# Second and third FFN: the first two blocks' activations split behind the third block's weights, and the second FFN's gates scaled behind the last low halves

## The chip, the cores and the metric

The kernel runs on one core of a Trainium2 chip. The metric is the device time of one execution in microseconds (us); lower is better. The time before is 2227.34 us, the median of three runs (2226.12 to 2228.6).

## The reference, cut to what matters

A trunk of four layers works on `x`, 512 positions of 1024 channels in float32. Each layer adds a mixer (S5, gated linear attention, differential attention, S5) and then an FFN with 2816 hidden channels. Only the FFN is touched here:

```python
def swiglu_ffn(h, w_gate_up, w_down):
    g, u = jnp.split(h @ w_gate_up, 2, axis=-1)
    return (jax.nn.silu(g) * u) @ w_down

for layer in range(DEPTH):
    ...
    x = x + mix
    h = rmsnorm(x, norm_ffn[layer])
    x = x + swiglu_ffn(h, ffn_w_gate_up[layer], ffn_w_down[layer])
```

The function `ffn` has an argument `l`, the layer from 0 to 3. The second and third FFN are `l == 1` and `l == 2`.

## The kernel before, in words

**High and low halves.** Every float32 operand of a large product is kept as a high half, rounded to the type that TensorE reads fast, and a low half, the rest. A product is three matmuls: high with high, high with low, low with high. A weight tile (128 partitions x 1024 elements, 512 KB) is staged by a DMA, cast to its high half by ScalarE (`high`, L420), and VectorE subtracts that from the weight to make the low half (`low`, L428). So each weight tile costs one ScalarE and one VectorE instruction before its products can run in full: the first two matmuls of a product need only the high half, the third needs the low one. Five pairs of halves (`whl`) exist at a time.

**A block.** The hidden channels are cut into 11 blocks of 256. A block's gate and up products are made with seven half-sized products instead of eight (`seven_block`, L729). Each product is 24 matmuls of 256 columns (L594), and its left operand is one of the prepared `side` tiles or `sides`. The names in a plan are the products and what is done with their sums: `one` starts a sum in PSUM bank `a`, and `one_out` (L800, ScalarE) copies it to the tile `r1`; `two` goes to bank `d` and `two_out` (L807, VectorE) adds it to `r1`; `five` and `five_out` (L821) make `r5` from bank `c`; `six` adds to bank `a`, once `one_out` has read it, and `six_out` (L835) copies it to `r2`; `seven` adds to `a`, once `six_out` has read it, and `seven_out` (L845) subtracts it from `r5`; `three` adds to `c`, and `three_out` (L852, L853) makes the gated `r1`; `four` adds to `a`. `scale1` and `gate2` (L770) multiply a gate by the rows' norms, `silu1` and `gate2` (L773) apply SiLU, `times` (L865) multiplies with `r5`. `add` (L824) adds one staged quarter of the weights to another, since `six` and `four` use sums: `add22` and then `high1`, `low1` make the operand of `six`, `add21` and then the last halves (`highF`, `lowF`) that of `four`.

**Activations.** Last, `parts` (L867) splits `r1` and `r5` into the high and low halves that the product with `w_down` reads: a ScalarE cast (L877) and a VectorE subtraction (L878) for each. In the third FFN the rows are permuted (`turn`), and each is done in two instructions of half the size. `parts` is also the last reader of `r1`.

**Buffers.** The tiles `r1` have two buffers (tag `r1`), the others three (tag `glu`, both at L734). PSUM has four banks for `a` and `c` and two for `d`.

**Order.** Blocks 1 and 2 ("a" and "b" in the plans) go side by side by a plan, a list of steps written by hand. Blocks 3 to 11 go one by one through the loop at the end of `ffn`. Block 3 is `blocks[2]`. After each group of blocks (4, 4 and 3) the loop `gemm_b` multiplies with `w_down`. Within this order a scheduler that runs when the program is built sets the final order of the instructions on each engine; every engine then runs its own list strictly in that order and waits by semaphores. `issue_after(ins)` binds what is traced under it to stand behind `ins` on the engine of `ins` alone. Weight loads are issued from SyncE, and loads that add to a staged quarter from GpSimd (L759); both wait for free buffers.

Second and third FFN are not `glued`: block 3's first products come out of the loop and not out of a plan, and in the loop `gate2`, `times` and `parts` of blocks 1 and 2 are traced ahead of block 3's steps.

Of the kernel before, what the change touches and what calls it, by code (L numbers as in the profile page):

```python
# [69 lines left out]
class Left:  # L70
# [4 lines left out]
    early = False  # L75
# [79 lines left out]
class Sides(Left):  # L155
# [4 lines left out]
    early = True  # L160
# [180 lines left out]
class Trunk:  # L341
# [544 lines left out]
    def ffn(self, l, left, after=None, turn=False, aside=None, small=None):  # L886
# [7 lines left out]
        with self.tc.tile_pool(name=f"ffn{l}", bufs=1, reuse_waits="tile") as fp:  # L894
# [3 lines left out]
            glued = l in (0, 3)  # L898
# [8 lines left out]
            blocks = [self.seven_block(fp, slots, left, wgu, b, turn, na, glued) for b in range(FFN_HIDDEN // 256)]  # L907
# [27 lines left out]
            if l == 1:  # L935
                a = plan.index("seven_out:b")
                plan = plan[:a] + """
                    seven_out:b scale1:a silu1:a scale1:b silu1:b add21a high22 low22 three:b highFa add21b lowFa highFb
                    lowFb four:a four:b three_out:a three_out:b
                """  # L940

            def turned():
# [3 lines left out]
            def loads(b=blocks[2]):  # L946
                for w in ("direct", "room1", "room22", "room21", "summed"):
                    b[w]()
# [22 lines left out]
            for nb in (4, 4, 3) if na == 4 else (3, 3, 3, 2):  # L971
                acts = []
                for n in range(b0, b0 + nb):
                    b = blocks[n]
                    if not glued and n < 2:
                        if l == 2 and n == 0:
                            loads()
                            blocks[2]["split"]("1")
                        if l == 2 and n == 1:
                            for step in ("one", "one_out", "five", "five_out"):  # L980
                                blocks[2][step]()
                            blocks[2]["add"]("22")
                            blocks[2]["split"]("1")
                        for step in ("gate2", "times"):
                            b[step]()
                    if n > 2 or l == 1 and n == 2:
                        loads(b)
                        for step in ("one", "one_out", "five", "five_out"):
                            b[step]()
                        b["add"]("22")  # L990
                    if n > 1:
                        for step in ("six", "six_out", "two", "two_out", "scale1", "silu1", "seven", "seven_out", "three", "three_out"):
                            b[step]()
                        b["add"]("21")
                        for step in ("four", "gate2", "times"):
                            b[step]()
                    with self.tc.issue_after(behind["low"].ins) if glued and n < 2 else nullcontext():
                        acts.append(b["parts"]())
                stat = lambda k, part, t: acts[k // 2][:, part, k % 2, t * P : (t + 1) * P]
                if b0 + nb == 11:  # L1000
                    if l == 0:
                        nxt = Sides(self, after, None, i["gla_w_in"][0], lambda half, b: GLA_COLS[b] + half * 256, True)
                    else:
                        nxt = (Chunks if turn else Last if l == 3 else Left)(self, after)
                for d in range(2):
                    tail = 4 if d == 1 and b0 + nb == 11 else 0
                    self.gemm_b(stat, wd, 2 * nb, d * 512, self.add_x(d, nxt, r), k0=2 * b0, tail=tail, jobs=jobs,
                                behind=None if d or l == 0 else dict(self.last),
                                ahead=(lambda: self.gla_ahead(nxt)) if tail and l == 0 else None,
                                middle=(lambda: nxt.total("3")) if tail and l == 0 else None)  # L1010
                b0 += nb
# [1916 lines left out]
```

## Time and profile before

| what | value |
|---|---|
| median of three runs | 2227.34 us |
| profiled execution, its own time | 2228.83 us |
| its span, first to last instruction | 2227.1 us |
| granted TensorE clock, mean | 0.998 |
| VectorE busy | 1631.7 us (73%) |
| ScalarE busy | 1145.4 us (51%) |
| second FFN, end of the plan and blocks 3 and 4 | about 800 to 856 us |
| third FFN, the same | about 1424 to 1470 us |

The profiled execution took 2228.83 us, of which 2227.1 lie between the first and the last instruction. Its rows are read so: the start in us from the span's start, the duration, the engine (PE is TensorE's matmuls, DVE VectorE, ACT ScalarE, POOL GpSimd), the line, the operation, out<-in by the program's names, the size, how often it stands in this row, and in brackets how long the engine stood idle before it and for whom. A matmul's duration includes its way through the array, so two starts tell more than one duration.

### The profile page before, as it was taken

How to read it: one execution, taken by the hardware profiler on the slowest of the kernel's cores; microseconds unless marked ns; L12 is line 12 of the kernel's file. 1: busy time of each engine (PE TensorE's matmuls, PEld its weight loads, DVE VectorE, ACT ScalarE, POOL GpSimd, SP SyncE). 2: the span in 40 equal slices, each digit the busy share in tenths (PEclk: the TensorE clock that was granted, in tenths of full speed). 3: DMA queues.
4: the chain of work that ended last, by engine and by line, in shares of the span. 5: the costliest groups of instructions: out<-in, count | busy, mean ns of one | idle time of the engine just before them, and what ended most of it. 6: DMA issues, size and time to landing. Idle time of an engine off the chain costs nothing.

```text
span 2227.1 us, 38431 instructions
## 1 busy us (share of the span) xinstructions
PE 2166.7 (97%) x15409; PEld 1964.6 (88%) x15409; DVE 1631.7 (73%) x2504; ACT 1145.4 (51%) x1844; POOL 332.2 (15%) x443
## 2 busy tenths in 40 slices
PE   6999999999999999999999999999999999999998
PEld 5888989989988898999888888999998888989997
DVE  9965878777988597876745676967766965957675
ACT  8644635444665465564435675644544234635343
POOL 3401142440210010100002221100000001101000
PEclk9999999999999999999999999999999999999999
DMA  4357667664863676764238455975631646856532
GB/s 93 64 173 179 174 156 188 178 172 157 187 149 114 160 193 164 178 187 124 95 130 167 108 133 150 252 193 143 180 94 48 171 142 152 208 152 170 162 76 76
DMA packets 309220, 333.75 MB, mean 150 GB/s; under 512 B 70452, under 2 KB 253008, under 8 KB 308914
## 3 DMA queue, kind: packets, MB, share of 16 engines
q1 hardware_dynamic: 239010, 239.07, 35.0%
q0 software_dynamic: 70032, 92.23, 22.0%
q8 instruction: 121, 1.98, 0.4%
q14 instruction: 57, 0.47, 0.1%
HBM read 297.29 MB, written 18.75 MB: 142 GB/s over the span
## 4 chain that ended last, share of the span: by engine, by line
PE 79%; DVE 10%; ACT 5%; issue 3%; DMA 1%; POOL 1%; SPq 0%; DVEq 0%; POOLq 0%; ACTq 0%
PE a L594 20%; PE acc L448 11%; PE acc L450 11%; PE acc L449 11%; PE c L594 10%; PE d L594 6%; DVE whl L428 2%; PE y L1670 2%; ACT whl L420 2%; PE acc L1706 2%; PE op L2711 1%; PE s L2678 1%; PE tp L117 1%; PE V L1626 1%; PE acc L2766 1%
## 5 line engine op out<-in xcount | busy, mean ns | idle before, releaser
L428 DVE TENSOR_TENSOR whl<-wst,whl 128x1024 fp32r<-128x1024 f32 x260 | 316.4, 1222 | 214.9 <-ACT whl L420 213.5
L594 PE MATMUL a<-side,whl 128*128 128x256 f32 x3240 | 393.4, 278 | 7.2 <-DVE whl L428 6.8
L420 ACT CAST whl<-wst 128x1024 fp32r<-128x1024 f32 x260 | 272.1, 1052 | 239.3 <-PE acc L450 152.8
L594 PEld LDWEIGHTS a<-side,whl 128*128 128x128 f32 x3240 | 379.6, 188 | 10.4 <-DVE whl L428 8.4
L448 PE MATMUL acc<-whl,act 128*128 128x512 f32 x704 | 275.8, 392 | 0.0
L449 PE MATMUL acc<-whl,act 128*128 128x512 f32 x704 | 274.5, 390 | 0.0
L450 PE MATMUL acc<-whl,act 128*128 128x512 f32 x704 | 274.5, 390 | 0.0
L594 PE MATMUL c<-side,whl 128*128 128x256 f32 x2160 | 261.4, 277 | 2.1 <-DVE whl L428 1.6
L594 PEld LDWEIGHTS c<-side,whl 128*128 128x128 f32 x2160 | 253.1, 188 | 2.9 <-DVE whl L428 2.0
L428 DVE TENSOR_TENSOR whl<-slot,whl 128x1024 fp32r<-128x1024 f32 x105 | 127.7, 1221 | 61.3 <-ACT whl L420 60.7
L448 PEld LDWEIGHTS acc<-whl,act 128*128 128x128 f32 x704 | 132.2, 188 | 27.9 <-DVE x L576 0.5
L450 PEld LDWEIGHTS acc<-whl,act 128*128 128x128 f32 x704 | 132.2, 188 | 27.7
L449 PEld LDWEIGHTS acc<-whl,act 128*128 128x128 f32 x704 | 132.2, 188 | 26.4
L420 ACT CAST whl<-slot 128x1024 fp32r<-128x1024 f32 x105 | 109.9, 1052 | 83.8 <-PE acc L450 44.6
L594 PE MATMUL a<-sides,whl 128*128 128x256 f32 x1080 | 132.6, 278 | 1.8 <-DVE whl L428 1.1
L594 PE MATMUL d<-sides,whl 128*128 128x256 f32 x1080 | 131.7, 278 | 1.6 <-ACT whl L420 1.6
L420 ACT CAST whl<-halves 128x1024 fp32r<-128x1024 f32 x87 | 91.0, 1051 | 80.3 <-DVE halves L824 31.0
L594 PEld LDWEIGHTS a<-sides,whl 128*128 128x128 f32 x1080 | 128.0, 188 | 3.1 <-DVE whl L428 1.4
L428 DVE TENSOR_TENSOR whl<-halves,whl 128x1024 fp32r<-128x1024 f32 x87 | 105.7, 1221 | 34.1 <-ACT whl L420 33.7
L594 PEld LDWEIGHTS d<-sides,whl 128*128 128x128 f32 x1080 | 127.7, 188 | 2.1 <-ACT whl L420 2.1
L759 POOL DMA_DIRECT2D wst<-in_ffn_w_gate_up_dram x44 | 57.0, 1296 | 446.1 <-DMA wst<-in_ffn_w_gate_up_dram 179.3
L877 ACT CAST act<-r 128x512 fp32r<-128x512 f32 (+1 forms) x110 | 66.1, 642 | 101.3 <-DVE r L853 83.7
(530 smaller groups left out, 4025.2 us busy)
## 6 DMA issues: line engine op xcount, KB each, us to landing
wst<-in_ffn_w_gate_up_dram SPq DMA_DIRECT2D x88, 512.0 KB, 4.8
wst<-in_ffn_w_down_dram SPq DMA_DIRECT2D x88, 512.0 KB, 4.6
slot<-in_ffn_w_gate_up_dram SPq DMA_DIRECT2D x69, 512.0 KB, 6.0
wst<-in_ffn_w_gate_up_dram POOLq DMA_DIRECT2D x44, 512.0 KB, 6.0
halves<-in_ffn_w_gate_up_dram SPq DMA_DIRECT2D x42, 512.0 KB, 6.8
wst<-in_s_w_glu_dram SPq DMA_DIRECT2D x32, 512.0 KB, 4.9
wst<-in_diff_w_qkv_dram SPq DMA_DIRECT2D x24, 512.0 KB, 4.1
slot<-in_ffn_w_gate_up_dram POOLq DMA_DIRECT2D x18, 512.0 KB, 8.5
```

Source lines behind the costliest of these rows:

```text
L117: tr.nc.tensor.transpose(p[:, j], h[:, j * P : (j + 1) * P], tr.ident[:])
L420: self.last["high"] = self.nc.scalar.copy(hl[:, 0], w[:])
L428: self.last["low"] = self.nc.vector.tensor_tensor(hl[:, 1], w[:], hl[:, 0].bitcast(F32), op=ALU.subtract)
L448: mm(out, lh, rh, start=first, stop=False)
L449: mm(out, lh, rl, start=False, stop=False)
L450: self.last["mm"] = mm(out, ll, rh, start=False, stop=last)
L594: mm(o, *two, start=first and not (j or k or n), stop=k == 3 and n == 2, skip_group_check=True,)
L759: nc.gpsimd.dma_start(w[:], left.quarter(*plus, b), accum_op=ALU.add)
L877: self.last["act high"] = nc.scalar.copy(dst[:, 0, j], src[:, j])
L1626: mm(V[kk][z][:, bs(b)], inm[:, z, bs(b)], U[:, bs(b)], start=True, stop=True)
L1670: mm(yb[:, b], q[:, j, b], om[:, j // 2, bs(b)], start=False, stop=j == 3)
L1706: mm(accs[t][:], zT[:, m // 2, kk, t * P : (t + 1) * P], hl[:, m % 2, kk % 2], start=kk == 0 and m == 0, stop=kk == KT - 1 and m == 2,)
```

## The change

Two things are moved, and nothing is added or left out. In the second FFN's plan `scale1` and `silu1` of both blocks go behind the last low halves (`lowFb`). In the second and third FFN `parts` of blocks 1 and 2 is traced behind block 3's `four`, and bound on VectorE behind block 3's low halves: in the second FFN behind the last of them (that of `four`), in the third FFN block 1's behind that of `seven` and block 2's behind the last.

```diff
             if l == 1:
                 a = plan.index("seven_out:b")
                 plan = plan[:a] + """
-                    seven_out:b scale1:a silu1:a scale1:b silu1:b add21a high22 low22 three:b highFa add21b lowFa highFb
-                    lowFb four:a four:b three_out:a three_out:b
+                    seven_out:b high22 add21a low22 three:b highFa lowFa add21b highFb lowFb scale1:a silu1:a four:a
+                    scale1:b silu1:b four:b three_out:a three_out:b
                 """
...
                     if n > 1:
                         for step in ("six", "six_out", "two", "two_out", "scale1", "silu1", "seven", "seven_out", "three", "three_out"):
                             b[step]()
+                            if step == "seven":
+                                early = self.last["low"]
                         b["add"]("21")
-                        for step in ("four", "gate2", "times"):
+                        b["four"]()
+                        if n == 2 and not glued:
+                            with self.tc.issue_after(early.ins if l == 2 else self.last["low"].ins):
+                                acts.append(blocks[0]["parts"]())
+                            with self.tc.issue_after(self.last["low"].ins):
+                                acts.append(blocks[1]["parts"]())
+                        for step in ("gate2", "times"):
                             b[step]()
+                    if not glued and n < 2:
+                        continue
                     with self.tc.issue_after(behind["low"].ins) if glued and n < 2 else nullcontext():
                         acts.append(b["parts"]())
```

What the built programs hold shows at three places. The first is VectorE (DVE) in the second FFN, right behind `seven_out:b`. `r_8202` and `r_8216` are `r1` of blocks 1 and 2, `lent` holds the quarters that become the operands of `four:a` and `four:b`. Before:

```order
L770 TENSOR_TENSOR r_8202<-r_8202,R 128x512
L770 TENSOR_TENSOR r_8216<-r_8216,R 128x512
L824 TENSOR_TENSOR lent<-lent,slot_8119 128x1024
L241 TENSOR_TENSOR side_8117<-halves,side_8117 128x1024
L824 TENSOR_TENSOR lent<-lent,slot_8120 128x1024
L428 TENSOR_TENSOR whl<-lent,whl 128x1024 x2
```

The same place on VectorE in the changed program:

```order
L824 TENSOR_TENSOR lent<-lent,slot_8119 128x1024
L241 TENSOR_TENSOR side_8117<-halves,side_8117 128x1024
L428 TENSOR_TENSOR whl<-lent,whl 128x1024
L824 TENSOR_TENSOR lent<-lent,slot_8120 128x1024
L428 TENSOR_TENSOR whl<-lent,whl 128x1024
L770 TENSOR_TENSOR r_8202<-r_8202,R 128x512
L770 TENSOR_TENSOR r_8216<-r_8216,R 128x512
```

The two gate scalings moved from the head of this row to its end, and the first low half no longer stands behind the second sum.

The second place is ScalarE (ACT) in the second FFN, around block 3's `one_out`. `r_8641` before and `r_8631` now are block 3's `r1`, `r_8304` and `r_8374` are `r5` of blocks 1 and 2. Before:

```order
L877 CAST act<-r_8304 128x2x256
L773 ACTIVATE g_8595<-g_8595 128x512
L800 COPY r_8641<-a 128x512
L877 CAST act<-r_8374 128x2x256
L420 CAST whl<-halves 128x1024
L420 CAST whl<-slot_8121 128x1024
L821 COPY r_8671<-c 128x512
L420 CAST whl<-wst 128x1024
L420 CAST whl<-halves 128x1024 x2
L835 COPY r_8701<-a 128x512
```

And in the changed program, from the same cast of `r_8304` on:

```order
L877 CAST act<-r_8304 128x2x256
L420 CAST whl<-halves 128x1024
L773 ACTIVATE g_8590<-g_8590 128x512
L420 CAST whl<-slot_8121 128x1024
L420 CAST whl<-wst 128x1024
L821 COPY r_8661<-c 128x512
L420 CAST whl<-halves 128x1024
L877 CAST act<-r_8374 128x2x256
L420 CAST whl<-halves 128x1024
L420 CAST whl<-wst 128x1024
L420 CAST whl<-halves 128x1024
L800 COPY r_8631<-a 128x512
```

Block 3's `one_out` moved from ahead of all casts of block 3's later weights to behind them, and behind two casts of block 4. It now waits, by its semaphores, for the VectorE split of block 1's `r1`, whose buffer it takes over; before it waited only for `one`.

The third place is VectorE in the third FFN, behind `three_out` of block 2. `r_14416` and `r_14430` are `r1` of blocks 1 and 2, `r_14518` and `r_14596` their `r5`. Before:

```order
L853 TENSOR_TENSOR r_14430<-r_14430,r_14653 128x512
L878 TENSOR_TENSOR act<-r_14416,act 128x64x4
L865 TENSOR_TENSOR r_14518<-g_14820,r_14518 128x512
L878 TENSOR_TENSOR act<-r_14416,act 128x64x4
L428 TENSOR_TENSOR whl<-wst,whl 128x1024
L878 TENSOR_TENSOR act<-r_14518,act 128x64x4 x2
L824 TENSOR_TENSOR halves<-halves 128x1024
L878 TENSOR_TENSOR act<-r_14430,act 128x64x4 x2
L428 TENSOR_TENSOR whl<-halves,whl 128x1024
L428 TENSOR_TENSOR whl<-slot_14331,whl 128x1024
L770 TENSOR_TENSOR g_14894<-a,R 128x512
L428 TENSOR_TENSOR whl<-wst,whl 128x1024
```

The same place on VectorE in the changed program:

```order
L853 TENSOR_TENSOR r_14430<-r_14430,r_14653 128x512
L428 TENSOR_TENSOR whl<-wst,whl 128x1024
L865 TENSOR_TENSOR r_14518<-g_14820,r_14518 128x512
L824 TENSOR_TENSOR halves<-halves 128x1024
L428 TENSOR_TENSOR whl<-halves,whl 128x1024
L428 TENSOR_TENSOR whl<-slot_14331,whl 128x1024
L824 TENSOR_TENSOR halves<-halves,slot_14331 128x1024
L428 TENSOR_TENSOR whl<-wst,whl 128x1024
L428 TENSOR_TENSOR whl<-halves,whl 128x1024 x2
L878 TENSOR_TENSOR act<-r_14416,act 128x64x4 x2
L878 TENSOR_TENSOR act<-r_14518,act 128x64x4 x2
L878 TENSOR_TENSOR act<-r_14430,act 128x64x4
```

All five low halves of block 3 from `one` on that are still open there come first, and the split activations (L878) behind them. Here too `one_out` of block 3 now waits for the split of block 1's `r1`.

On TensorE the products of block 3 stand in the order one, five, six, two, seven, three, four before, with the first two matmuls of some pulled ahead. In the changed program they stand as one, five, two, three, six, seven, four, with `one` of block 4 cut into pieces between six, seven and four, and with two matmuls of block 4's `five` ahead of `six` in the second FFN.

## The prediction, as it was put on record

> **What bounds the kernel now.** The page's first part says which engine carries the time:
>
> ```profile
> PE 2166.7 (97%) x15409; PEld 1964.6 (88%) x15409; DVE 1631.7 (73%) x2504; ACT 1145.4 (51%) x1844; POOL 332.2 (15%) x443
> ```
>
> TensorE is busy for 97% of the span. A change that adds no matmul and removes none can only move the time by the moments in which TensorE waits. So I next read the windows around the two places, each line with the window, its length and the busy time of each engine:
>
> ```profile
> 800.00:830.00 30.00, 26.68 (x226) 25.87 (x225) 28.93 (x35) 19.07 (x24) 5.15 (x4) 1.00 1.00 246
> 830.00:860.00 30.00, 30.00 (x249) 29.32 (x248) 23.10 (x28) 14.28 (x21) 2.57 (x2) 1.00 0.73 195
> 1430.00:1450.00 20.00, 17.48 (x144) 16.69 (x144) 19.89 (x27) 13.30 (x19) 3.86 (x3) 1.00 1.13 281
> ```
>
> In the first and the third, VectorE is busy 28.93 of 30 us and 19.89 of 20 while TensorE has holes of 3.3 and 2.5 us. Here VectorE is the bound, and the order of its list decides. Behind it (830 to 860) TensorE is never idle, so what is lost or won before stays to the end.
>
> TensorE's timeline shows the holes. The second FFN, from `four` of blocks 1 and 2 on:
>
> ```profile
> 807.84 0.39 PE L594 MATMUL a<-side,whl 128*128 128x256 f32 x2
> 809.96 5.50 PE L594 MATMUL a<-side,whl 128*128 128x256 f32 x46 [1.73 <-DVE whl L428]
> 815.30 2.88 PE L594 MATMUL a<-sides,whl 128*128 128x256 f32 x24
> 818.02 0.39 PE L594 MATMUL c<-side,whl 128*128 128x256 f32 x2
> 819.51 2.78 PE L594 MATMUL c<-side,whl 128*128 128x256 f32 x22 [1.10 <-DVE whl L428]
> 822.33 0.50 PE L594 MATMUL a<-side,whl 128*128 128x256 f32 x2
> 823.28 0.50 PE L594 MATMUL d<-sides,whl 128*128 128x256 f32 x2 [0.44 <-ACT whl L420]
> 823.62 2.76 PE L594 MATMUL a<-side,whl 128*128 128x256 f32 x22
> 826.22 2.70 PE L594 MATMUL d<-sides,whl 128*128 128x256 f32 x22
> 828.76 2.88 PE L594 MATMUL a<-side,whl 128*128 128x256 f32 x24
> 831.48 2.88 PE L594 MATMUL c<-side,whl 128*128 128x256 f32 x24
> ...
> 856.00 0.39 PE L448 MATMUL acc<-whl,act 128*128 128x512 f32 x1
> ```
>
> Undisturbed, 24 matmuls take 831.48 - 828.76 = 2.72 us, 0.113 each. What a start lies later than the one before it plus its matmuls is lost: 809.96 - 807.84 - 0.23 = 1.89 before the third matmul of `four:a`, 1.26 before the third of block 3's `five`, then 0.33, 0.72 and 0.11 around `six` and `two`. Sum **4.31 us**. The last row is the first matmul with `w_down`. The third FFN, from block 3's `one` on:
>
> ```profile
> 1428.92 0.39 PE L594 MATMUL a<-sides,whl 128*128 128x256 f32 x2
> 1429.47 2.86 PE L594 MATMUL c<-side,whl 128*128 128x256 f32 x22 [0.16 <-DVE r L852]
> 1433.47 2.86 PE L594 MATMUL a<-sides,whl 128*128 128x256 f32 x22 [1.15 <-DVE whl L428]
> 1436.17 0.40 PE L594 MATMUL c<-side,whl 128*128 128x256 f32 x2
> 1437.77 0.50 PE L594 MATMUL d<-sides,whl 128*128 128x256 f32 x2 [1.21 <-ACT whl L420]
> 1438.26 3.09 PE L594 MATMUL a<-side,whl 128*128 128x256 f32 x24
> 1441.18 2.73 PE L594 MATMUL d<-sides,whl 128*128 128x256 f32 x22
> 1443.76 0.39 PE L594 MATMUL c<-side,whl 128*128 128x256 f32 x2
> 1444.31 3.00 PE L594 MATMUL a<-side,whl 128*128 128x256 f32 x24 [0.17 <-ACT r L835]
> ```
>
> In the same way 0.32, 1.51, 0.21, 1.37, 0.26 and (at 1444.31) 0.32: **3.99 us**. So all that there is to win at both places is about 8.3 us.
>
> **The change part by part.** It removes no instruction, so each list is walked with durations of before. They come from these rows of VectorE, ScalarE and GpSimd:
>
> ```profile
> 802.89 0.68 DVE L845 TENSOR_TENSOR r<-r,a 128x512 f32<-128x512 f32 x1
> 803.49 1.28 DVE L770 TENSOR_TENSOR r<-r,R 128x512 f32<-128x512 f32 x2
> 804.69 1.22 DVE L824 TENSOR_TENSOR lent<-lent,slot 128x1024 f32<-128x1024 f32 x1
> 826.86 2.35 DVE L428 TENSOR_TENSOR whl<-halves,whl 128x1024 fp32r<-128x1024 f32 x2
> 829.13 0.68 DVE L807 TENSOR_TENSOR r<-r,d 128x512 f32<-128x512 f32 x1
> 1429.93 0.68 DVE L853 TENSOR_TENSOR r<-r,r 128x512 f32<-128x512 f32 x1
> 1430.53 0.62 DVE L878 TENSOR_TENSOR act<-r,act 128x256 fp32r<-128x256 f32 x1
> 1431.07 0.68 DVE L865 TENSOR_TENSOR r<-g,r 128x512 f32<-128x512 f32 x1
> 809.83 1.05 ACT L420 CAST whl<-wst 128x1024 fp32r<-128x1024 f32 x1
> 810.79 1.04 ACT L420 CAST whl<-halves 128x1024 fp32r<-128x1024 f32 x1
> 817.82 0.63 ACT L773 ACTIVATE g<-g 128x512 f32<-128x512 f32 x1 [0.64 <-DVE g L770]
> 818.35 0.57 ACT L800 COPY r<-a 128x512 f32<-128x512 f32 x1
> ...
> 1438.58 1.06 ACT L420 CAST whl<-wst 128x1024 fp32r<-128x1024 f32 x1
> 1425.07 1.31 POOL L759 DMA_DIRECT2D wst<-in_ffn_w_gate_up_dram x1 [0.43 <-DVE whl L428]
> ```
>
> A full weight tile on VectorE holds the next one back by (829.13 - 826.86) / 2 = 1.14 and gives its result after 1.22; a 512 one 0.60 and 0.68; the half-sized split 0.54 and 0.62. On ScalarE a cast holds 0.96 and gives its result after 1.05, a 512 one 0.53 and 0.57 to 0.63. Between engines I add 0.03.
>
> *Second FFN, `four` of blocks 1 and 2.* VectorE is free at 803.49 as before. Sum a to 804.71, `side` at 804.63, cast a on ScalarE to 805.79, low a 805.82 to 807.04, sum b 806.96 to 808.18, cast b to 809.26, low b 809.29 to 810.51. TensorE reaches `four:a` at 807.84 and `four:b` at 810.56: both halves are there. **The 1.89 us go.** The two scalings that stood ahead (2 x 0.60) now stand behind, where `three_out`, which needs them, is waited for by nobody at once.
>
> *Second FFN, block 3.* TensorE is early now: `one` at 813.28, `five` at 816.00. On VectorE, 810.43: three 512 instructions, low of `one` 812.23, four 512 ones, low of `five` 815.77 to 816.99. The third matmul of `five` comes at 817.03 instead of 816.23: 0.80 lost. It ends at 819.52. `two` stands next. Its cast on ScalarE is queued behind the cast for `six`, which waits for `add22` (VectorE 817.51 to 818.73), and a SiLU: 818.76, 819.72, 820.25 to 821.30. `two` starts at 821.33: 1.81 lost. Its low half is behind that of `six` and a `times`: 821.58 to 822.80, third matmul 822.83: 1.27 lost. `two` and `three` run through to 828.04. Then block 4's first pieces wait for their casts, which stand behind the cast for `four`, and that for `add21` (VectorE 824.99 to 826.21): 826.24, 827.20, 828.16. Two matmuls at 828.28, two at 829.24. ScalarE copies `one_out` at 829.18 (it also waits for the split of block 1's `r1`, 828.46 to 829.14), to 829.76, and `six` starts at 829.79: 0.24 + 0.74 + 0.33. `six` ends 832.51; two pieces of block 4's `one` wait for their low half to 833.29: 0.81; before `four` about 0.1. The sum is 0.80 + 1.81 + 1.27 + 1.31 + 0.81 + 0.1 = **6.1 us**, against 4.31: **1.8 us lost**. The gain at `four` is eaten, since an earlier TensorE meets the same VectorE and ScalarE lists.
>
> *Third FFN.* The two lists are alike up to VectorE's 1429.93. Then low of `one` 1430.53 to 1431.75, where it was a split with the low half far behind. TensorE has 11 matmuls of `five` (0.32 lost ahead, as before), which end at 1430.72; third of `one` 1431.78: 1.06 lost. `five` ends 1435.74. `times` 1431.67, `add22` 1432.27 to 1433.49, its cast to 1434.57, the low of `six` 1434.60, of `two` 1435.74 to 1436.96; third of `two` 1436.99: 1.02 lost. `add21` 1436.88, lows of `seven`, `three` (1439.16 to 1440.38) and `four` (1440.30): third of `three` 1440.41, 0.70 lost. Only now the splits of `r1`, 1441.44 and 1441.98 to 1442.60; ScalarE's `one_out` to 1443.20, `six` 1443.23: 0.55 lost. Then two splits of `r5`, one of block 2's `r1` and a gate (1444.14 to 1444.82), SiLU, `two_out`, a split, `times` to 1446.55, and on ScalarE two casts of block 2's `r5` ahead of `six_out`: 1446.58, 1447.04, 1447.50 to 1448.10. `seven` could start at 1446.41 and starts at 1448.13: 1.72 lost. `four` waits 0.35 for `seven_out`. Sum 0.32 + 1.06 + 1.02 + 0.70 + 0.55 + 1.72 + 0.35 = **5.7 us** against 3.99: **1.7 us lost**.
>
> The sum: 1.8 + 1.7 = 3.5 us. The profiled execution (2228.83, span 2227.1) would take 2232.3, its span 2230.6; it stands 1.49 above the median, so the median would be 2227.34 + 3.5 = **2230.8 us**. Loads hang on the freed tiles and move with the lists; SyncE issues the same loads, some in another order, and none of the walked steps waits for one. No new kind of work is in the change, so no price is unknown; unknown is how far each of the 15 new joints is off. Counted over all 144 matmuls from 807.84 to 828.76, the second FFN lost 20.92 - 16.32 = 4.60, 0.29 more than its six joints show, 0.05 for each. Between exact and 0.1 more at each new joint the sum is 3.5 to 5.0 us. I take 3.5, since the old joints hide as much and only the difference counts.
>
> A rule of the Trainium skill speaks against my spacing: its page "VectorE: DVE Perf Modes", section "The DRAIN you can't avoid", says that a VectorE instruction starts only when the one before has left the pipe. By the row of two low halves (2.35 for two of 1.22) the second starts 0.08 before the first has ended, so the trace does not bear this out for plain successors. By the rule the sum would be about 5 us (the rival without overlap, below).
>
> **The rivals.** *It is faster.* If block 3's `one_out` in the second FFN ended before TensorE is through `three` at 828.04, 1.7 us sooner than walked, and ScalarE's casts with it, the three waits for low halves (1.89, 1.26 and, in the third FFN, 1.51) would go and none come: 2227.34 - 4.66 = 2222.7. For it: these are the waits that the rows name. Against it: the two buffers of `r1`, and VectorE's full windows; the work is only moved. *Half of that:* only the 1.89 is kept and the rest comes out even, 2225.5 to 2229. *More is lost.* In the third FFN ScalarE's cast of the operand of `seven` (L420 at 1438.58 before) now follows `five_out`, which follows the end of `five` (1435.74), and comes at 1436.3, over 2 us earlier. Its tile is filled by the load that GpSimd issues at 1425.07, and these take
>
> ```profile
> DMA to landing us min/median/max: 6.7/9.9/10.9
> ```
>
> from issue to landing between 1405 and 1450, so it has landed by 1425.07 + 10.9 = 1435.97, 0.3 us ahead. If it lands 2 us late, that cast and the one for `three` behind it hold TensorE for 1 us or more; with 0.1 more at each joint (1.5 us) this gives 2231.8 to 2236. *No overlap on VectorE.* If in the new order each VectorE instruction waited out the 0.08 us that the next one now overlaps, the some 20 in the third FFN's chain up to `six_out` would bring `seven` 20 x 0.08 = 1.6 us later: 2232.4. The pair of low halves above speaks against it. *The clock falls.* Both windows show a granted clock of 1.00 with a hole of 1.89 in them. Were it to fall to a half for some microseconds, each 24 matmuls would take another 2.72 us: with two or more such groups 2236 and above. The Trainium skill, page "TensorE: Matmul & The Clock Gate", section "A second HAM failure mode: psum-queue depth-cycling", says that many short pauses between groups of matmuls can make the clock swing; in this trace it did not. That the change does not do what it says is ruled out by the rows of the built programs.
>
> **How the numbers follow.** 0.2% is 4.45 us and about what a measurement of this kernel can tell from no change. Chances: the forecast (2229 to 2231.8) 0.53; half the gain (2225.5 to 2229) 0.14; more lost (2231.8 to 2236) 0.24; no overlap 0.01; faster 0.06; the clock 0.02. So faster 0.06, within 0.2% 0.53 + 0.14 = 0.67, slower 0.24 + 0.01 + 0.02 = 0.27. The range leaves out the faster case, the clock and the ends of the two beside the forecast: 2226.5 to 2234.5.
>
> **What would show it.** Right: TensorE runs `four` of blocks 1 and 2 in the second FFN without a hole; then holes before `two` (for ScalarE's cast, then for VectorE's low half) of about 1.8 and 1.3; `six` waits for ScalarE's L800 in both FFNs, and that for L878; in the third FFN `seven` waits some 1.7 for L835. TensorE's first matmul with `w_down`, at 856.00 in the second FFN before, comes 1.8 later. Wrong: `six` not waiting for L800, or a wait on a load in either window.

## The result, and the profile after

The changed kernel takes **2233.16 us** (median of 10 runs, 2230.62 to 2236.82) against 2227.74 for the kernel before (10 runs, 2226.12 to 2229.92). The medians lie 5.4 us apart. The ratio of the two kernels' times is put at 1.0020 with a 95% interval of 1.0012 to 1.0028, so the change loses 2.7 to 6.2 us. Forecast was a loss of 3.5, to a median of 2230.8.

The first part of the page of the profiled execution (2234.14 us, span 2232.4), then the windows of two stretches shown of before:

```profile
PE 2171.0 (97%) x15409; PEld 1968.3 (88%) x15409; DVE 1632.0 (73%) x2504; ACT 1145.9 (51%) x1844; POOL 331.9 (15%) x443
...
800.00:830.00 30.00, 26.00 (x214) 24.86 (x214) 27.06 (x33) 16.75 (x22) 3.87 (x3) 1.00 0.98 234
1430.00:1450.00 20.00, 16.18 (x130) 14.99 (x129) 18.70 (x26) 13.86 (x21) 5.16 (x4) 1.00 1.13 303
```

The counts of instructions are those of before. In 800 to 830 TensorE runs 12 matmuls fewer than before (214 against 226) and in 1430 to 1450 it runs 14 fewer. The engine that was full, VectorE, is now **less** busy there: 27.06 against 28.93 us, and 18.70 against 19.89. It did not lose time to more work. It waited.

TensorE in the second FFN, from `four` on:

```profile
806.06 5.64 PE L594 MATMUL a<-side,whl 128*128 128x256 f32 x48
811.54 3.11 PE L594 MATMUL a<-sides,whl 128*128 128x256 f32 x24
814.49 0.39 PE L594 MATMUL c<-side,whl 128*128 128x256 f32 x2
815.41 2.86 PE L594 MATMUL c<-side,whl 128*128 128x256 f32 x22 [0.53 <-DVE whl L428]
819.77 0.50 PE L594 MATMUL d<-sides,whl 128*128 128x256 f32 x2 [1.50 <-ACT whl L420]
821.30 2.86 PE L594 MATMUL d<-sides,whl 128*128 128x256 f32 x22 [1.03 <-DVE whl L428]
...
826.83 0.41 PE L594 MATMUL a<-sides,whl 128*128 128x256 f32 x2
828.18 0.50 PE L594 MATMUL c<-side,whl 128*128 128x256 f32 x2 [0.93 <-ACT whl L420]
828.66 3.00 PE L594 MATMUL a<-side,whl 128*128 128x256 f32 x24
...
856.36 0.39 PE L448 MATMUL acc<-whl,act 128*128 128x512 f32 x1
```

The two `four` run without a hole, as 48 matmuls in one row. Starts less the matmuls between them give 0.69 before the third matmul of `five`, 1.87 and 1.30 around the start of `two` (bank `d`), and 1.12 before block 4's `five`. From the first matmul of `four` to the first one with `w_down` it took 856.36 - 806.06 = 50.30 us. Before it took 856.00 - 807.84 = 48.16, so **2.1 us** are lost here. (The whole trace runs 1.8 us ahead at this place: the trace of before has a stretch of half clock at 262.67, and this one has it later. More of that below.)

TensorE in the third FFN, from block 3's `one` on:

```profile
1430.12 0.39 PE L594 MATMUL a<-sides,whl 128*128 128x256 f32 x2
1430.69 1.54 PE L594 MATMUL c<-side,whl 128*128 128x256 f32 x11 [0.18 <-DVE r L852]
1433.02 2.78 PE L594 MATMUL a<-sides,whl 128*128 128x256 f32 x22 [0.79 <-DVE whl L428]
...
1438.32 2.81 PE L594 MATMUL d<-sides,whl 128*128 128x256 f32 x22 [0.81 <-DVE whl L428]
...
1444.55 3.00 PE L594 MATMUL a<-side,whl 128*128 128x256 f32 x24 [0.27 <-ACT r L800]
...
1447.62 0.39 PE L594 MATMUL a<-sides,whl 128*128 128x256 f32 x2
1449.40 3.00 PE L594 MATMUL a<-side,whl 128*128 128x256 f32 x24 [1.40 <-ACT r L835]
...
1474.15 0.39 PE L448 MATMUL acc<-whl,act 128*128 128x512 f32 x1
```

`six` (1444.55) waits for L800 and `seven` (1449.40) for L835. To the first matmul with `w_down` it is 1474.15 - 1430.12 = 44.03. The row of before that answers is

```profile
1471.45 0.39 PE L448 MATMUL acc<-whl,act 128*128 128x512 f32 x1
```

and 1471.45 - 1428.92 = 42.53, so **1.5 us** are lost here. Below, "the second FFN" and "the third FFN" mean these two stretches, from the same first to the same last matmul.

Now VectorE. These are all of its waits in the two windows, two of them with the sum ahead, and in the third FFN alike:

```profile
805.24 1.22 DVE L824 TENSOR_TENSOR lent<-lent,slot 128x1024 f32<-128x1024 f32 x1
807.66 1.23 DVE L428 TENSOR_TENSOR whl<-lent,whl 128x1024 fp32r<-128x1024 f32 x1 [1.20 <-ACT whl L420]
...
818.28 1.22 DVE L428 TENSOR_TENSOR whl<-halves,whl 128x1024 fp32r<-128x1024 f32 x1 [0.59 <-ACT whl L420]
...
823.44 1.21 DVE L824 TENSOR_TENSOR halves<-halves,slot 128x1024 f32<-128x1024 f32 x1
825.76 1.22 DVE L428 TENSOR_TENSOR whl<-halves,whl 128x1024 fp32r<-128x1024 f32 x1 [1.11 <-ACT whl L420]
```

```profile
1433.49 1.22 DVE L824 TENSOR_TENSOR halves<-halves 128x1024 f32<-128x1024 f32 x1
1435.90 1.23 DVE L428 TENSOR_TENSOR whl<-halves,whl 128x1024 fp32r<-128x1024 f32 x1 [1.20 <-ACT whl L420]
```

All four have one form, the second with one scaling (L770) in between: VectorE makes a sum (L824), ScalarE casts it (L420), VectorE makes the low half (L428). The three hang on one another, and VectorE stands idle for the length of the cast (1.05 us and the ways there and back) unless something else stands in between. Before, the scalings and splits stood in between: 1.0 us of waits in 800 to 830 and none in 1430 to 1450, against 2.9 and 1.2 now. This is the first candidate for the cause. The second is block 3's `one_out` (L800):

```profile
1442.72 2.75 DVE L878 TENSOR_TENSOR act<-r,act 128x256 fp32r<-128x256 f32 x5
```

```profile
1443.91 0.58 ACT L800 COPY r<-a 128x512 f32<-128x512 f32 x1 [1.66 <-DVE act L878]
```

In the third FFN ScalarE is free and waits 1.66 us for the split of block 1's `r1` (the first two of the five), whose buffer `one_out` needs.

### The profile page after: what moved, and what is told of

Same layout as the page of the kernel before. It is cut to its first block, busy times and chain, and to the rows that moved or that the text cites. A ratio compares the mean times of both kernels' runs of the same rounds, so it can differ in the third digit from the quotient of the medians.

```text
span 2232.4 us, 38426 instructions
## 1 busy us (share of the span) xinstructions
PE 2171.0 (97%) x15409; PEld 1968.3 (88%) x15409; DVE 1632.0 (73%) x2504; ACT 1145.9 (51%) x1844; POOL 331.9 (15%) x443
## 4 chain that ended last, share of the span: by engine, by line
PE 80%; DVE 9%; ACT 5%; issue 2%; DMA 2%; POOL 1%; SPq 0%; DVEq 0%; POOLq 0%; ACTq 0%
PE a L594 20%; PE acc L448 11%; PE acc L450 11%; PE acc L449 11%; PE c L594 10%; PE d L594 5%; DVE whl L428 2%; PE y L1680 2%; ACT whl L420 2%; PE acc L1716 2%; PE op L2721 1%; PE s L2688 1%; PE tp L117 1%; PE V L1636 1%; PE acc L2776 1%
## 5 line engine op out<-in xcount | busy, mean ns | idle before, releaser
L428 DVE TENSOR_TENSOR whl<-wst,whl 128x1024 fp32r<-128x1024 f32 x260 | 316.4, 1222 | 215.2 <-ACT whl L420 213.5
L420 ACT CAST whl<-wst 128x1024 fp32r<-128x1024 f32 x260 | 272.2, 1052 | 241.5 <-PE acc L450 154.7
L428 DVE TENSOR_TENSOR whl<-slot,whl 128x1024 fp32r<-128x1024 f32 x105 | 127.7, 1221 | 61.0 <-ACT whl L420 60.9
L420 ACT CAST whl<-slot 128x1024 fp32r<-128x1024 f32 x105 | 109.9, 1052 | 83.5 <-PE acc L450 44.6
L428 DVE TENSOR_TENSOR whl<-halves,whl 128x1024 fp32r<-128x1024 f32 x87 | 105.7, 1221 | 37.8 <-ACT whl L420 37.6
L420 ACT CAST whl<-halves 128x1024 fp32r<-128x1024 f32 x87 | 90.8, 1051 | 78.1 <-DVE halves L824 28.9
```

Of the source, the lines that this page charges most:

```text
L420: self.last["high"] = self.nc.scalar.copy(hl[:, 0], w[:])
L428: self.last["low"] = self.nc.vector.tensor_tensor(hl[:, 1], w[:], hl[:, 0].bitcast(F32), op=ALU.subtract)
```

## The experiments

Three theories are told apart. **The filler**: the moved instructions filled VectorE's waits behind the sums. **The buffer**: the late split of `r1` makes `one_out` late, and `six` and `seven` behind it. **The clock**: the granted clock falls for a few microseconds.

### One part of the change at a time

Only the plan (`e1_plan`):

```diff
-                    seven_out:b scale1:a silu1:a scale1:b silu1:b add21a high22 low22 three:b highFa add21b lowFa highFb
-                    lowFb four:a four:b three_out:a three_out:b
+                    seven_out:b high22 add21a low22 three:b highFa lowFa add21b highFb lowFb scale1:a silu1:a four:a
+                    scale1:b silu1:b four:b three_out:a three_out:b
```

> Only the second FFN's plan is changed (the scalings of blocks 1 and 2 behind the last low half); the split activations stay where they were. Theory 1, the filler: a sum on VectorE, ScalarE's cast of it and the low half of it need one another, so VectorE stands idle for about 1.2 us between sum and low half unless something else stands there; the moved instructions were what stood there. Then VectorE waits 1.2 us between the sum b and its low half, the hole of 1.89 us at the product four of block 1 is gone, and a walk through the lists with the durations of before brings the first matmul with w_down (856.00 before) 0.6 us later: the total is 0.3 to 0.9 us over before. Theory 2, the buffer: what costs is block 3's one_out, which waits for the late split of r1. Here that split is early, so most of the 1.89 us is kept: 1 to 1.9 us under before. Theory 3, the clock: the windows move by less than 0.5 us, and the total follows the number of stretches of half clock, some 1.5 us each.

Measured: 2230.61 us against 2229.76, ratio 1.0005 (0.9996 to 1.0014). The trace has no hole at `four`, but a longer one before the third matmul of block 3's `five`:

```profile
816.60 0.39 PE L594 MATMUL c<-side,whl 128*128 128x256 f32 x2
820.52 4.19 PE L594 MATMUL c<-side,whl 128*128 128x256 f32 x22 [3.53 <-DVE whl L428]
824.54 0.39 PE L594 MATMUL a<-side,whl 128*128 128x256 f32 x2
```

The second FFN loses 1.76 us. Of this some 1.5 are clock: the 22 matmuls from 820.52 take 4.02 us, where 22 x 0.113 is 2.49. Without it 0.2 to 0.3 are left, near the 0.6 of the walk. The 1.89 us are not kept, although `one_out` is early here (818.08), so the buffer alone does not explain the loss.

Only the splits of the second FFN (`e3_parts_second`) and only those of the third (`e4_parts_third`), both with the old plan; here the second, the third has `l == 2`:

```diff
-                        if n == 2 and not glued:
+                        if n == 2 and l == 1:
...
-                    if not glued and n < 2:
+                    if l == 1 and n < 2:
                         continue
```

> Only the split activations of the second FFN are moved; the plan and the third FFN are as before. Theory 1, the filler: VectorE idles ahead of the low half of the operand of six and that of four, where the splits stood; the walk gives 1.2 us later at the first matmul with w_down, total 0.9 to 1.5 over before. Theory 2, the buffer: all that the second FFN loses in the changed kernel comes from here, with the 1.89 us at four still standing: 2.1 + 1.89 = about 4 us over before. Theory 3, the clock: no more than 0.5 us at the first matmul with w_down.

> Only the split activations of the third FFN are moved; the second FFN is as before. Theories 1 and 2 both expect what the changed kernel shows there, 1.6 to 1.8 us over before at the third FFN's first matmul with w_down, and as much in the total if the clock is alike. Theory 3, the clock: 5.4 us of the changed kernel are mostly stretches of half clock that go with any change of order, so the total is 1.7 us plus some 1.5 for each such stretch more than before.

Measured: 2230.73 (ratio 1.0004, 0.9995 to 1.0012) and 2231.41 (1.0003, 0.9994 to 1.0012), against 2229.76. By the traces the one loses 1.28 us in the second FFN and nothing in the third (-0.17), the other 0.00 in the second and 1.74 in the third. The terms sit where the change sits, at the sizes that the walk gives (1.2 and 1.6). Where a kernel leaves a stretch as it was, its trace differs from that of before by 0.00, -0.17 and, in the third FFN of the plan alone, -0.22 us, so differences of some 0.2 us say nothing. By the times alone none of the three parts can be told from no change; their medians sum to a loss of 3.5.

The changed kernel beside them (`c1_after`), and two traces more of it (`c2_after`, `c3_after`):

> The changed kernel once more, beside the others on one chip. Without more stretches of half clock than before: 2.1 + 1.75 = 3.9 us over before. Theory 3, the clock: 5 us or more over before again, with stretches of half clock in the trace that before has not at the same places; if they belong to the change they are at the same places as in the first trace of it (1281, 1752 and 1943 us), if they come and go, at others.

> The changed kernel for another trace. The stretches of half clock last 3.41 us each, and the three of its first trace begin 138.0 and 56.0 times 3.41 us apart. Theory 3a: the clock is judged in fixed stretches of 3.41 us whose beginning is random from run to run, and a stretch in which TensorE was busy for less than about half is followed by one of half clock. Then the pauses at 819 to 822 us (3.2 of 4.3 us idle) bring one at about 820 to 825 in some traces and not in others, and all starts within one trace lie a whole number of 3.41 us apart. Theory 3b: the stretches at 262, 1281, 1752 and 1943 have nothing to do with the change, and the one at 823 was an exception: none at 820 here.

> The changed kernel for a further trace, as the one before: by theory 3a a stretch of half clock at 820 to 825 in about half of such traces, by theory 3b none.

Measured: 2233.61 against 2229.76 (ratio 1.0018, 1.0010 to 1.0027), then single runs of 2233.38 and 2232.47. The four traces of the changed kernel lose in the second FFN 2.14, 3.64, 3.67 and 1.96 us, in the third 1.50, 1.58, 1.43 and 1.76. The two with 3.6 have a stretch of half clock right there. Windows of `c2_after`, cut at its beginning (PEclk is the third column from the end):

```profile
819.16:822.57 3.41, 0.88 (x6) 0.66 (x6) 3.38 (x4) 3.41 (x5) 0.00 (x0) 1.00 0.79 132
822.57:825.98 3.41, 3.41 (x19) 3.41 (x18) 2.98 (x3) 1.34 (x3) 1.28 (x1) 0.50 0.35 57
825.98:829.40 3.42, 3.42 (x31) 3.42 (x30) 2.73 (x4) 1.70 (x2) 0.00 (x0) 1.00 1.04 218
```

In the 3.41 us ahead TensorE was busy for 0.88, because two holes came right after one another; then the clock is halved for 3.41 us (19 matmuls for 31), though TensorE is busy all through. The stretches at other places are as short, follow pauses that both kernels have, and change from trace to trace: 262.67 in the one of before, 1280.70, 1751.74 and 1942.89 in the first of the changed kernel, none of these in the second. The three starts of that trace lie 471.04 and 191.15 apart, 138.0 and 56.0 times 3.413, so the cuts between the stretches run on by themselves, and it is chance on which side of a cut a pause falls. The two traces of the changed kernel without half clock at 820 agree: in the first a cut falls at 819.90, between the two holes, and the 3.41 us on its two sides hold 1.91 and 2.38 us of TensorE's work. So the fixed stretches of theory 3a are borne out, and 3b's "none at 820" falls in one trace of two (`c2_after` has one, `c3_after` none). The row ahead of the stretch in the trace of before, and that of the second trace of the changed kernel (`c1_after`):

```profile
259.26:262.67 3.41, 1.81 (x12) 1.50 (x13) 3.41 (x6) 1.42 (x2) 1.30 (x1) 1.00 0.20 22
```

```profile
819.56:822.97 3.41, 1.81 (x13) 1.61 (x14) 3.41 (x5) 3.41 (x5) 0.64 (x1) 1.00 0.45 75
```

TensorE was idle for 1.6 of 3.41 us, in two pieces in the second case (1.59 and 1.03, of which a part lies in the row), and half clock followed. It need not: theory 3a's "less than about half" is not the whole rule. With all 13 traces cut at this spacing, from 25 to 2200 us, each of the five full-clock stretches with 1.25 us of work or less is followed by half clock, but of those with 1.5 to 2.1 us only 11, and 73 are not. Ahead of 1280.70 in the first trace of the changed kernel the work was 1.56 us, with half clock behind it; at the same place in `c2_after` it was 1.57, with full clock. What decides there stays open. The Trainium skill, page "TensorE: Matmul & The Clock Gate", section "Part 1: The HAM clock gate (the "warmup" mystery)", gives a free-running window of 3413 ns, which agrees with the length and the spacing here. Its section "Why this matters for your kernels" advises against pauses over some 3 us; by these rows, pauses of half that length can do it when they fall into one window.

### The buffer against the filler

Two kernels differ by one exchange: block 1's split of `r1` stands early, right behind `add22`, and that of its `r5` late (`h2_r1_early`), or the other way round (`h6_r5_early`). In the second FFN their lists on VectorE are the same but for this, up to the last low half of block 3; TensorE's and ScalarE's lists, and in the third FFN VectorE's too, come out of the scheduler in another order. `parts` is told which tiles to split and which tile to fill. Here in the second FFN, in the third alike:

```diff
                         b["add"]("22")
+                        if n == 2:
+                            half = blocks[0]["parts"](("r1",))
...
-                                acts.append(blocks[0]["parts"]())
+                                acts.append(blocks[0]["parts"](("r5",), half))
```

> The changed kernel, but in both FFNs block 1's split of r1 (one ScalarE cast and one VectorE subtraction; in the third FFN two of each, half as large) is traced right behind the sum add22 of block 3; the split of block 1's r5 and those of block 2 stay late. Theory 2, the buffer: r1 of block 1 is free early, so block 3's one_out is early, six needs not stand behind two and three, and the walk of the lists gives 1.7 us less than before at the second FFN's first matmul with w_down and 0.3 more at the third's: total 1.4 under before. Theory 1, the filler: one VectorE instruction of 0.68 (two of 0.62) fills a part of the 0.59 and 1.20 us in which VectorE waits for the cast behind add22, so about 0.6 us better than the changed kernel in each FFN: total some 2.6 over before.

> As the one with r1 early, but the split of block 1's r5 is early and that of its r1 stays late: the same instructions of the same size in the same places on VectorE, only the buffer of r1 is free late. Theory 1, the filler: the same time as the one with r1 early. Theory 2, the buffer: as slow as the changed kernel; the walk gives 1.1 over before in the second FFN and 2.2 in the third, total 3.3 over before, 4.7 over the one with r1 early.

Measured: 2230.47 and 2233.76 against 2229.07, ratios 1.0008 (0.9999 to 1.0016) and 1.0020 (1.0011 to 1.0029). They are 3.3 us apart, where the filler expects 0 and the buffer 4.7. The second FFN shows how, with r1 early and then with r5 early:

```profile
819.90 3.04 PE L594 MATMUL a<-side,whl 128*128 128x256 f32 x24 [1.11 <-ACT r L800]
```

```profile
821.18 0.50 PE L594 MATMUL d<-sides,whl 128*128 128x256 f32 x2 [2.06 <-ACT whl L420]
823.07 0.60 PE L594 MATMUL c<-side,whl 128*128 128x256 f32 x2 [1.39 <-ACT whl L420]
823.47 4.26 PE L594 MATMUL d<-sides,whl 128*128 128x256 f32 x22
```

With r1 early `six` follows `five` and covers the time in which the casts and low halves of `two` are made. With r5 early `six` comes only behind `two` and `three`, and TensorE meets casts that are not there yet. The second FFN gains 1.58 in the one and loses 3.05 in the other (about 1.5 with the half clock taken off: the row of 22 matmuls at 823.47 lasts 4.26 us, such a row in full clock 2.8). The walk had 1.7 less and 1.1 more. So the buffer matters, with some 3 us in the second FFN, by way of the order that it allows. In the third FFN the one with r5 early loses 2.61, where the walk had 2.2.

The third FFN of `h2_r1_early` is a miss: 4.17 us lost where 0.3 were expected. So it was traced again (`h2_again`: 2235.08, single run).

> The kernel with block 1's r1 split early, for another trace. Its first one had 6.83 us of half clock from 1443.89 on and lost 4.2 us in the third FFN where the walk gives 0.3. By theory 3a the third FFN's pauses at 1436 to 1444 bring half clock in this trace too if they fall into one stretch of 3.41 us, and without it the third FFN loses less than 1.2 us; by theory 3b the 4.2 us are lost again without half clock.

It loses 4.71 there, again with 6.83 us of half clock (from 1449.78 on), and gains 1.10 in the second FFN, 0.5 less than the first trace. The first trace, TensorE, ScalarE and the windows:

```profile
1444.65 0.80 PE L594 MATMUL c<-side,whl 128*128 128x256 f32 x2 [2.92 <-ACT whl L420]
1446.53 4.95 PE L594 MATMUL a<-side,whl 128*128 128x256 f32 x24 [1.08 <-ACT r L835]
```

```profile
1443.56 1.04 ACT L420 CAST whl<-halves 128x1024 fp32r<-128x1024 f32 x1 [6.03 <-DMA halves<-in_ffn_w_gate_up_dram]
```

```profile
1440.48:1443.89 3.41, 1.25 (x11) 1.05 (x9) 1.31 (x3) 0.33 (x1) 0.06 (x1) 1.00 1.13 300
1443.89:1447.30 3.41, 1.56 (x5) 1.27 (x6) 2.13 (x3) 3.17 (x6) 1.23 (x1) 0.50 1.17 247
1447.30:1450.72 3.42, 3.42 (x18) 3.42 (x17) 3.42 (x6) 1.33 (x3) 1.28 (x1) 0.50 1.17 281
```

Block 3 is through so early that ScalarE, in its fixed order, waits 6.03 us for the load of a block 4 weight, with block 3's SiLU and `six_out` queued behind it. (In the changed kernel the same cast comes at 1449.78 and waits for nothing.) The hole then brings two stretches of half clock. Both traces have the pair of stretches, so it is hardly chance. How much of the 4.2 us each of the two has was not measured apart. So in the third FFN the buffer and the filler are not told apart by experiment; there the trace of the changed kernel alone speaks for both, with 1.66 us of wait at `one_out` and 1.20 on VectorE.

The filler by itself: the changed kernel with the scalings between the second sum and its low half (`f1_scale_between`).

```diff
-                    seven_out:b high22 add21a low22 three:b highFa lowFa add21b highFb lowFb scale1:a silu1:a four:a
-                    scale1:b silu1:b four:b three_out:a three_out:b
+                    seven_out:b high22 add21a low22 three:b highFa lowFa add21b highFb scale1:a silu1:a scale1:b silu1:b lowFb four:a
+                    four:b three_out:a three_out:b
```

> The changed kernel, but the scalings of both blocks stand between the second sum (add21 of block 2) and its low half, where VectorE waits 1.20 us for ScalarE's cast; the split activations stay late in both FFNs. Theory 1, the filler: the wait is filled at no cost to four, everything behind it on VectorE comes 1.2 us sooner, and the walk gives 0.3 under before in the second FFN (2.1 better than the changed kernel) and still 1.6 over in the third: total 1.3 over before. Theory 2, the buffer: nothing changes for one_out, which waits for the split of r1, so 0.6 us better than the changed kernel at most: 3 us over before.

Measured: 2232.07 against 2229.07, ratio 1.0012 (1.0003 to 1.0021). The total lies at the buffer's 3, but the trace speaks for the filler: the second FFN loses 0.35 us, where the filler's walk had 0.3 gained, the buffer 1.4 lost or more, and the changed kernel loses 2.0 to 2.1 without half clock. `one_out` still waits here for the split of `r1` (1.19 us, to 827.92). Of VectorE's three waits one is left:

```profile
820.37 1.23 DVE L428 TENSOR_TENSOR whl<-halves,whl 128x1024 fp32r<-128x1024 f32 x1 [0.57 <-ACT whl L420]
```

The third FFN loses 1.77, as expected. The two sum to 2.1, inside the interval of the ratio (0.7 to 4.7 us). So neither theory holds alone: each remedy by itself takes back most of what the second FFN loses.

### Both remedies together

`g4_gaps_filled` is the changed kernel with one scaling behind each cast in the plan, block 1's splits behind `add22` and block 2's behind `add21`, not bound any more:

```diff
-                    seven_out:b high22 add21a low22 three:b highFa lowFa add21b highFb lowFb scale1:a silu1:a four:a
-                    scale1:b silu1:b four:b three_out:a three_out:b
+                    seven_out:b high22 add21a low22 three:b highFa scale1:a silu1:a add21b lowFa highFb scale1:b silu1:b lowFb four:a
+                    four:b three_out:a three_out:b
...
                         b["add"]("22")
+                        if n == 2:
+                            acts.append(blocks[0]["parts"]())
...
-                        b["four"]()
-                        if n == 2 and not glued:
-                            with self.tc.issue_after(early.ins if l == 2 else self.last["low"].ins):
-                                acts.append(blocks[0]["parts"]())
-                            with self.tc.issue_after(self.last["low"].ins):
-                                acts.append(blocks[1]["parts"]())
+                        if n == 2 and not glued:
+                            acts.append(blocks[1]["parts"]())
+                        b["four"]()
```

> Both remedies together: one scaling between each sum and its low half in the second FFN's plan, all split activations of block 1 right behind add22 of block 3 and those of block 2 behind add21, in both FFNs. Both theories expect it below before: the walk gives 2.4 us less in the second FFN and 0.9 less in the third, total 3.4 under before. Theory 3, the clock: fewer and shorter pauses of TensorE around 820 us, so no stretch of half clock there and a mean granted clock no lower than that of before; the time could also come out level with before, if what limits is something that the walk does not hold.

Measured: **2226.69 us** against 2229.07, ratio 0.9987 (0.9978 to 0.9996): faster than before, and below both medians of the changed kernel. The windows and the second FFN's ends:

```profile
800.00:830.00 30.00, 29.01 (x248) 28.30 (x248) 30.00 (x37) 18.39 (x24) 4.31 (x4) 1.00 1.00 245
1430.00:1450.00 20.00, 19.77 (x167) 19.29 (x166) 20.00 (x26) 12.37 (x19) 3.37 (x3) 1.00 1.15 291
```

```profile
806.63 0.39 PE L594 MATMUL a<-side,whl 128*128 128x256 f32 x2
807.56 5.50 PE L594 MATMUL a<-side,whl 128*128 128x256 f32 x46 [0.55 <-DVE whl L428]
...
852.34 0.39 PE L448 MATMUL acc<-whl,act 128*128 128x512 f32 x1
```

VectorE has no wait left in either window (30.00 of 30, 20.00 of 20). The second FFN takes 852.34 - 806.63 = 45.71, 2.4 us less than before, as the walk gave; the third gains 1.0. That is 3.4 together, as forecast, where the medians differ by 2.4. What theory 3 expected of the clock came true in the trace, which has no half clock before its last 3 us, but it is the fastest of the eleven executions (2223.78). Over all of them the mean granted clock is 0.9980, against 0.9986 for the 33 of before, so it is lower; why was not found. Among executions of the same clock, rounded to 0.001, the kernel is 2.3 to 5.8 us faster than before.

## Why the prediction was right, and what it left out

**The bound** was read rightly: the order of VectorE's list decides in both windows.

**The second FFN.** Forecast 1.8 lost, measured 2.14 and 1.96 in the traces without half clock there. The 1.89 us at `four` went and came back as forecast: 0.69 for 0.80 at `five`, 1.87 and 1.30 for 1.81 and 1.27 at `two`, 1.12 and 0.25 for the 1.31 around block 4's pieces and `six`. One step was wrong in its reason and not in its size, and with it one of the signs named for "right": `one_out` did not wait for the split of `r1` here. That split, the first of three in the first row below, ended at 827.59 and not at 829.14; `one_out` came at 828.03 because of the cast of a block 4 weight ahead of it on ScalarE, and `six` started right behind it, at 828.66:

```profile
826.91 1.89 DVE L878 TENSOR_TENSOR act<-r,act 128x512 fp32r<-128x512 f32 x3
827.08 1.05 ACT L420 CAST whl<-halves 128x1024 fp32r<-128x1024 f32 x1 [0.39 <-ACT whl L420]
828.03 0.58 ACT L800 COPY r<-a 128x512 f32<-128x512 f32 x1
```

That cast starts 0.09 us behind the end of `three`'s matmuls (826.99), so by these times it waited for a pair of halves to come free and not for its load; the profile does not name it. That the scheduler put `one_out` behind that cast hangs on the buffer all the same, as the pair with r1 and r5 early shows.

**The third FFN.** Forecast 1.7, measured 1.43 to 1.76 in four traces, mean 1.57. The waits came where they were walked: 1.08 us for 1.06 before the third matmul of `one`, 0.97 for 1.02 at `two`, 0.54 for 0.70 at `three`, 0.55 for 0.55 at `six`. Here `six` waited for L800, that for L878, and `seven` 1.55 us (1.72 forecast) for L835. The profile names no wait of TensorE, VectorE or ScalarE on a load in either window.

**The sum.** 2.05 + 1.57 = 3.6 against 3.5. The time itself was met less well: 2233.16 lies inside the stated range, but above 2229 to 2231.8, where the forecast had put 0.53, and in the interval of "more lost" (0.24), whose reasons did not happen. What the sum left out is the clock. It was held to be no part of the forecast because both windows of before showed 1.00 with a hole of 1.89 in them, and so had a chance of 0.02. That reading of one trace failed. Outside the two windows that trace has a stretch of half clock itself, at 262.67, behind pauses that add up to 1.6 us, so "in this trace it did not" holds for the windows alone. And the new order puts holes of 1.87 and 1.30 us side by side, with two matmuls between them, and in two of four traces that brought 3.41 us of half clock, which cost 1.6 us each time. With half of that, 0.8, the loss is 4.4 us, beside the 4.5 and 4.0 of the two ratios. This may not be all of the clock: over the 11 executions of `c1_after` its mean is 0.9974, against 0.9983 for the 33 of before on the same chip, and 0.0009 of 2230 us is about 2 us. Most of the loss is not clock, though: executions of equal clock, rounded to 0.001, are 3.2 us apart at 0.998 (2 against 16) and 4.4 at 0.999 (3 against 14), though only 1.9 at 0.997 (3 against 2). The rival "the clock falls" had the mechanism and too high a price.

**The rivals that did not happen**: no late load, no 0.1 us at each joint, no missing overlap on VectorE (two low halves in a row take 2.35 us in the changed kernel too, at 1440.45). The faster case needed `one_out` to end before TensorE is through `three`. In the kernel with both remedies it ends at 818.42, ahead of `three` (827.82), and that kernel is faster, by less than the 4.66 us of that case.

## What to carry to other kernels

Work that is put off from a full engine is worth nothing if it was what filled that engine's waits; look first at what the instruction behind it waits for (sum, cast, low half), and leave something there. A tile with two buffers makes its last reader part of the next block's critical path, so the reader that frees a buffer goes first and its equals go last; look at the loads then, for in the second FFN this paid and in the third it ran into a load that had not landed. And pauses that are harmless one by one should not be pushed together: in the changed kernel the clock fell behind 3.41 us that held two short holes, where one of the two did not do it.

## What the runs showed of the hardware

The granted clock fell to 0.50 for 3.41 us (6.83 in both traces of the kernel with r1 early) at 64, 262, 282, 820 to 823, 1281, 1443, 1450, 1750 or 1943 us, not counting the last 8 us of each trace. Traces of one kernel share some places and not others: of the changed kernel's four, two have it at 823 and the other two at 1751. Each time it began behind 3.41 us in which TensorE was busy for no more than 2.1. The cost at 823 was 1.6 us; half of the length, 1.7, is the most that a full stretch can cost. That a place has such a pause does not mean that the clock falls in every trace: with 1.25 us of work or less it fell each time (5 of 5), with 1.5 to 2.1 in 11 of 84, and what decides between these was not found.
